# Three quarters of the first feed-forward product computed from seven block products instead of eight

## The chip, the cores and the metric

The kernel runs on one core of a Trainium2 chip. The metric is the device time of one execution in microseconds (us), so less is better. The engines of the core are named as in the profile: PE (matrix products; PEld is its weight load), DVE (VectorE, elementwise work), ACT (ScalarE, activations, copies and casts), POOL (GpSimd) and SP (which only issues DMAs here). Each has a queue of its own and works it off in order; semaphores tie the queues together.

## What is computed

One inference step of a two-layer network on 640 tokens (128 prompt tokens and 512 sample tokens), D = 1024 and a feed-forward width of 4096. A layer is a mixer (one wide projection, four branches, their gates, an output projection) and then a feed-forward block:

```python
h = _rmsnorm(x, g_pre_ffn) * (1 + sc2) + sh2
f = jnp.square(jax.nn.relu(h @ w_ff1)) @ w_ff2
x = x + gt2 * _rmsnorm(f, g_post_ffn)
```

The scale, shift and gate vectors (`sc1`, `sh2`, `gt2` and so on) come from `silu(cond) @ w_ada + b_ada`, for two conditioning vectors.

## The kernel before

**Precision.** Every fp32 operand x of a product is split: `hi` is x cast to fp32r, `lo` is x - hi. A product is three matmuls: hi by hi, hi by lo, lo by hi (`mm3`, L205).

**Weights.** All weights of the two layers are cut into 264 units of 128x1024, 132 for each layer. A unit is fetched by SP into one of three raw buffers (`wr`), ACT casts it to `wh` (L160), DVE subtracts to get `wl` (L170). Four pairs of `wh`/`wl` (`N_SETS`) exist, so the unit in use and the three that follow it can be ready at once (`w_pump`, `w_low`, `w_next`, `w_done`).

**Feed-forward.** `ffn` (L1106) goes over the 4096 columns in four quarters c = 0 to 3. In a quarter, the "ff stage" makes 8 blocks of 128 columns, each in two halves of 320 tokens: 24 matmuls of 128x320 (8 blocks of the contraction by 3), then ACT takes Relu out of PSUM (L1117) and Square into `ghi` (L1118), and DVE squares again and subtracts to get `glo` (L1119, L1120). The "nat stage" (`natural`, L565) then multiplies the 1024 columns by `w_ff2`: 8 units of 30 matmuls of 128x512, the results added into `f` by DVE (L578). In quarter 0 the norm of the last tokens is still being finished inside the ff stage.

**Side work.** The conditioning products are done on DVE, a chunk of 512 columns at a time: 16 accumulations of 128x512 per chunk (L413, L415), 20 chunks in all, then an all-reduce over the partitions on POOL. They are a generator (`ada`), and so is other side work (convolution, pooling, attention). `tick(pe, dve)` is called after each group of matmuls: it adds `pe - dve` to a credit, and generators run as long as the credit is above zero. It then makes one `wl` (`w_low(1)`). `need` runs `ada` to the point where a given vector is there.

**What sets the order.** The program is written in the order of emission; each engine takes its instructions in that order (manual schedule). PSUM has two groups of four buffers (`mm` and `sd`). Tiles of 128x640 come from a pool of 27 (`T`).

Of the kernel before, what the change touches and what calls it, by code (L numbers as in the profile page):

```python
# [27 lines left out]
TICKS = 5  # L28
NAT_TICK = ((1.2, 0), (0.9, 0), (0.1, 0), (0.6, 0.6))
FF_DVE = 0.8  # L30
KN = {'l_pl': 2, 'ws': 0.0, 'l_brow': 2, 'l_red': 2, 'l_red2': 2, 'l_q': 2, 'l_last': 3, 'l_mean': 3, 'l_var': 3, 'l_rb': 4, 'l_ub': 2, 'sec': 0.5, 'gp': 0.1, 'bp': 0.75, 'qs': 2.0, 'qkv': 0, 'j0': -2, 'pv': 0.5, 'sc': 0.5, 'cv': 1.5}
# [38 lines left out]
class Kernel:  # L70
# [35 lines left out]
    def add(self, name, gen, unit, steps):  # L106
        self.sides.append(Side(name, gen, self.l * N_UNITS + unit, steps))
# [31 lines left out]
    def w_init(self):  # L139
        self.w_dma = 0  # L140
        self.w_split = 0
        self.w_at = 0
        self.w_live = 0
        self.w_raw = {}
        self.w_raw_live = 0
        self.w_late = []
        self.w_set = {}

    def w_pump(self, upto):
        nc = self.nc  # L150
        total = L * N_UNITS
        while self.w_split <= min(upto, total - 1) and self.w_live < N_SETS:
            i = self.w_split
            if i not in self.w_raw:
                self.w_low()
            self.w_fetch(i)
            raw = self.w_raw.pop(i)
            hi = self.wp.tile([128, 1024], F32R, tag="wh", name=self.nm("wh"), bufs=N_SETS)
            lo = self.wp.tile([128, 1024], F32R, tag="wl", name=self.nm("wl"), bufs=N_SETS)
            nc.scalar.copy(hi, raw)  # L160
            self.w_set[i] = (hi, lo)
            self.w_late.append((i, raw, hi, lo))
            self.w_split += 1
            self.w_live += 1

    def w_low(self, n=None, upto=None):

        while self.w_late and (n is None or n > 0) and (upto is None or self.w_late[0][0] <= upto):
            i, raw, hi, lo = self.w_late.pop(0)
            self.nc.vector.tensor_tensor(lo, raw, r32(hi), ALU.subtract)  # L170
            self.credit -= W_DVE
            self.w_raw_live -= 1
            self.w_fetch(i + N_RAW)
            n = None if n is None else n - 1

# [11 lines left out]
    def w_next(self):  # L187
# [3 lines left out]
        self.w_low(upto=i)  # L191
# [367 lines left out]
    def x_load(self, t, src, bufs=3):  # L559
# [5 lines left out]
    def natural(self, hi, lo, f, mode, ch=None):  # L565
# [5 lines left out]
        for n in range(2):  # L571
# [37 lines left out]
            for j in range(4):  # L609
                u, st = self.w_next()  # L610
                for t in range(NT):
# [5 lines left out]
                    self.tick(*NAT_TICK[j])  # L617
# [487 lines left out]

    def ffn(self, hi, lo, f, ch):  # L1106
        nc = self.nc
        for c in range(4):
# [13 lines left out]
            order = [(i, h) for i in range(8) for h in range(2)]  # L1122
            if c == 0:
# [264 lines left out]
```

## Time and profile before

| | us |
|---|---|
| three runs, lowest / median / highest | 2076.58 / 2079.00 / 2079.83 |
| the profiled execution | 2085.78 |
| its span, first to last instruction | 2083.9 |
| PE busy in the span | 2031.3 (97%) |
| DVE busy | 1305.9 (63%) |
| ACT busy | 787.1 (38%) |
| POOL busy | 286.3 (14%) |

The profiled execution lies 6.8 us above the median of the runs. PE's matmuls overlap, so its busy share says that matmuls were in flight, not that the array was at its peak. In the span, layer 0's feed-forward lies at 603 to 1062 us and layer 1's at 1621 to 2084. The stages of a quarter alternate: ff, nat, ff, nat.

### The profile page before, as it was taken

The page shows a single profiled execution, that of the slowest core. Times are in us where ns is not written, and L with a number is a line of the kernel's source. Part 1 is how long each engine was busy: PE and PEld are TensorE (multiplying, and loading weights), DVE is VectorE, ACT ScalarE, POOL GpSimd, SP SyncE. Part 2 cuts the span into 40 slices and gives each one's busy share as a digit, 9 for nine tenths or more (in the row PEclk, how much of TensorE's full clock was granted, in tenths as well). Part 3 has the DMA queues.
Part 4 walks back from the last instruction along what each step waited for, and adds up shares of the span by engine and source line. Part 5 has one row for each costly group of instructions (what it writes and reads, how often), then busy time and mean ns, then how long its engine had stood idle before and what let it go on. Part 6 is the DMA issues. An engine that isn't in the chain of part 4 may idle for free.

```text
span 2083.9 us, 30694 instructions
## 1 busy us (share of the span) xinstructions
PE 2031.3 (97%) x12368; PEld 1884.0 (90%) x12368; DVE 1305.9 (63%) x2293; ACT 787.1 (38%) x1538; POOL 286.3 (14%) x213
## 2 busy tenths in 40 slices
PE   7999999899999999999989999999999999999998
PEld 4999999899889898989889999889998889989896
DVE  4678785578678385656776898666434863333344
ACT  4433445433263241313354344455324523223231
POOL 1203001013231123121241030100001211000000
PEclk9999999999999999999999999999999999999999
DMA  7332121233434243343534222112224442222222
GB/s 298 121 111 79 63 67 35 86 117 122 152 130 164 92 148 126 102 137 123 168 115 134 71 75 72 56 53 96 72 72 152 135 138 81 80 72 78 74 103 80
DMA packets 77935, 221.41 MB, mean 106 GB/s; under 512 B 11224, under 2 KB 12248, under 8 KB 77792
## 3 DMA queue, kind: packets, MB, share of 16 engines
q1 hardware_dynamic: 48160, 164.00, 23.2%
q10 hardware_dynamic: 28096, 55.34, 8.0%
q8 instruction: 97, 1.59, 0.3%
q0 software_dynamic: 1536, 0.10, 0.2%
q14 instruction: 46, 0.38, 0.1%
HBM read 208.61 MB, written 10.80 MB: 105 GB/s over the span
## 4 chain that ended last, share of the span: by engine, by line
PE 83%; DVE 7%; ACT 5%; issue 2%; DMA 1%; POOL 1%; ACTq 0%; SPq 0%; DVEq 0%; POOLq 0%
PE nat L208 8%; PE nat L210 8%; PE nat L209 8%; PE ff L213 7%; PE ff L214 7%; PE ff L212 7%; PE gp L212 6%; PE gp L213 6%; PE gp L214 6%; PE sec L212 3%; PE sec L214 3%; PE sec L213 3%; PE bp L212 2%; PE bp L214 2%; PE bp L213 2%; DVE wl L170 2%
## 5 line engine op out<-in xcount | busy, mean ns | idle before, releaser
L170 DVE TENSOR_TENSOR wl<-wr,wh 128x1024 fp32r<-128x1024 f32 x264 | 349.8, 1328 | 215.9 <-ACT wh L160 215.5
L160 ACT CAST wh<-wr 128x1024 fp32r<-128x1024 f32 x264 | 274.2, 1045 | 369.5 <-PE nat L210 305.3
L212 PE MATMUL gp<-hhi,wh 128*128 128x320 f32 x1024 | 321.6, 314 | 3.1 <-ACT sg L1076 2.2
L213 PE MATMUL ff<-hlo,wh 128*128 128x320 f32 x1024 | 317.4, 310 | 3.9 <-DVE hlo L540 2.7
L213 PE MATMUL gp<-hlo,wh 128*128 128x320 f32 x1024 | 319.1, 312 | 0.0
L214 PE MATMUL gp<-hhi,wl 128*128 128x320 f32 x1024 | 318.9, 311 | 0.0
L214 PE MATMUL ff<-hhi,wl 128*128 128x320 f32 x1024 | 317.2, 310 | 1.3 <-DVE wl L170 1.3
L212 PE MATMUL ff<-hhi,wh 128*128 128x320 f32 x1024 | 317.5, 310 | 0.0
L208 PE MATMUL nat<-wh,ghi 128*128 128x512 f32 x640 | 252.9, 395 | 0.0
L209 PE MATMUL nat<-wl,ghi 128*128 128x512 f32 x640 | 252.3, 394 | 0.0
L210 PE MATMUL nat<-wh,glo 128*128 128x512 f32 x640 | 252.3, 394 | 0.0
L427 POOL PARTITION_ALL_REDUCE red<-acc x40 | 147.0, 3719 | 741.5 <-DVE acc L415 390.0
L415 DVE SCALAR_TENSOR_TENSOR acc<-wa,silu_c,acc 128x512 f32<-128x512 f32 x280 | 196.8, 759 | 7.9 <-DMA wa<-in_wada_dram 7.8
L212 PEld LDWEIGHTS gp<-hhi,wh 128*128 128x128 f32 x1024 | 195.1, 191 | 4.9 <-ACT sg L1076 2.4
L213 PEld LDWEIGHTS ff<-hlo,wh 128*128 128x128 f32 x1024 | 192.9, 188 | 5.3 <-issue 3.4
L213 PEld LDWEIGHTS gp<-hlo,wh 128*128 128x128 f32 x1024 | 194.7, 190 | 1.3
L214 PEld LDWEIGHTS gp<-hhi,wl 128*128 128x128 f32 x1024 | 194.7, 190 | 0.0
L214 PEld LDWEIGHTS ff<-hhi,wl 128*128 128x128 f32 x1024 | 192.8, 188 | 1.8 <-DVE wl L170 1.8
L212 PEld LDWEIGHTS ff<-hhi,wh 128*128 128x128 f32 x1024 | 192.8, 188 | 0.3
L1076 ACT ACTIVATE sg<-gp 128x320 f32<-128x320 f32 x128 | 55.5, 434 | 294.7 <-PE gp L214 276.9
L1119 DVE TENSOR_TENSOR r<-r 128x320 f32<-128x320 f32 x128 | 62.6, 489 | 156.6 <-ACT ghi L1118 156.5
L1117 ACT ACTIVATE r<-ff 128x320 f32<-128x320 f32 x128 | 56.0, 438 | 248.1 <-PE ff L214 231.3
(204 smaller groups left out, 3782.8 us busy)
## 6 DMA issues: line engine op xcount, KB each, us to landing
wr<-in_wu_dram SPq DMA_DIRECT2D x264, 512.0 KB, 3.2
wa<-in_wada_dram ACTq DMA_DIRECT2D x160, 256.0 KB, 3.1
wa<-in_wada_dram SPq DMA_DIRECT2D x16, 512.0 KB, 8.6
x<-x ACTq DMA_DIRECT2D x15, 512.0 KB, 3.3
x<-x SPq DMA_DIRECT2D x15, 512.0 KB, 5.6
x<-in_x_sample_dram SPq DMA_DIRECT2D x8, 512.0 KB, 6.8
gp<-in_g_post_dram ACTq DMA_DIRECT2D x16, 256.0 KB, 3.2
out_dram<-x SPq DMA_DIRECT2D x10, 256.0 KB, 2.0
```

The costliest lines, as they stand in the source:

```text
L160: nc.scalar.copy(hi, raw)
L170: self.nc.vector.tensor_tensor(lo, raw, r32(hi), ALU.subtract)
L208: mm(out, lhsT=xhi, rhs=whi, start=start, stop=False)
L209: mm(out, lhsT=xhi, rhs=wlo, start=False, stop=False)
L210: mm(out, lhsT=xlo, rhs=whi, start=False, stop=stop)
L212: mm(out, lhsT=whi, rhs=xhi, start=start, stop=False)
L213: mm(out, lhsT=whi, rhs=xlo, start=False, stop=False)
L214: mm(out, lhsT=wlo, rhs=xhi, start=False, stop=stop)
L415: nc.vector.scalar_tensor_tensor(acc[c], w[k], s, acc[c], ALU.mult, ALU.add)
L427: nc.gpsimd.partition_all_reduce(red[c], acc[c], 128, bass_isa.ReduceOp.add)
L1117: nc.scalar.activation(r, ps[:, :HALF], AF.Relu)
L1119: nc.vector.tensor_tensor(r, r, r, ALU.mult)
```

## The change

Quarter 0 stays as it is. In quarters 1 to 3, units are taken in pairs (u, u+1), that is two blocks of 128 columns. The tokens are cut in two (p and q, 320 each), the contraction in two (4 blocks of 128 each), the columns in two (u and u+1): a 2x2 by 2x2 block product. It is made from seven block products (12 matmuls each, so 84 for 96), with sums of weight blocks, sums of token blocks, and sums of the results.

- **Weights.** A pair becomes four sets (`w_init`, `self.parts`): A = unit u; B = unit u+1 with its left half replaced by left plus right; C = two running sums over u's buffer; D = half a set, the last running sum. The sums are made in place in the raw buffers by DVE, four additions of 128x512 (`"sums"`, `"add22"`, `"add21"`). Casts and subtractions become two of 1024 and three of 512 columns for a pair, where there were two of 1024.
- **Tokens.** `ffn_acts` makes three sums and one replacement in place for each of four blocks, as side work in the nat stage of quarter 0: 14 DVE instructions of 128x320 and four casts on ACT a block. They lie in tiles of the `x` pool, which grows from three to four buffers, and of the `T` pool.
- **Results.** `ffn_pairs` is the new ff stage. Seven DVE instructions of 128x320 and one ACT copy gather the products out of PSUM; then Relu, Square and cast of 128x640 on ACT, and one subtraction of 128x640 on DVE, for each of the two blocks.
- **Side work.** While `ffn_pairs` runs, the credit is held at -1, so no generator runs. In the nat stages of the feed-forward the credit is 1.39 a tick (`FF_TICK`). `ab2` and `ab1` are needed later, in `late`, in the middle of the nat stage.

```diff
+FF_TICK = ((1.39, 0), (1.39, 0), (1.39, 0), (1.39, 0.7))
...
+                elif u % 2 == FF0 % 2:
+                    plan = [[(ALL, g, ALL, "sums")], [(ALL, g + 1, ALL, None)],
+                            [(LEFT, g, LEFT, "add22"), (RIGHT, g, LEFT, "add21")], [(LEFT, g, LEFT, "free")]]
...
+            v(lo, raw, r32(hi), ALU.subtract)
             self.credit -= W_DVE
-            self.w_raw_live -= 1
-            self.w_fetch(i + N_RAW)
+            if then == "sums":
+                self.w_fetch(u + 1)
+                x, y = self.w_raw[u], self.w_raw[u + 1]
+                v(x[:, LEFT], x[:, LEFT], y[:, LEFT], ALU.add)
+                v(y[:, LEFT], y[:, LEFT], y[:, RIGHT], ALU.add)
+            elif then == "add22":
+                v(raw, raw, self.w_raw[u + 1][:, RIGHT], ALU.add)
+                self.w_drop(u + 1)
+            elif then == "add21":
+                v(raw, raw, self.w_raw[u][:, RIGHT], ALU.add)
+            elif then == "free":
+                self.w_drop(u)
...
-    def x_load(self, t, src, bufs=3):
+    def x_load(self, t, src, bufs=4):
...
-                    self.tick(*NAT_TICK[j])
+                    self.tick(*(NAT_TICK if ch else FF_TICK)[j])
...
+        def square(j, x):
+            nc.scalar.activation(x, x, AF.Relu)
+            nc.scalar.activation(x, x, AF.Square)
+            nc.scalar.copy(ghi[j], x)
+            late.append((j, x))
+
+        def low():
+            j, x = late.pop(0)
+            v(glo[j], x, r32(ghi[j]), ALU.subtract)
+
+        for pr in range(4):
+            U, R = self.T("u"), self.T("r")
+            ps = {}
+            for ns in ((1, 2), (7, 3), (5, 6), (4,)):
+                u, st = self.w_next()
+                for i, n in enumerate(ns):
+                    w = ps[n] = (self.sdps if n in (7, 3, 5) else self.mmps)("ffp")[:, :HALF]
+                    for k in range(4):
+                        c = slice(i * 512 + k * 128, i * 512 + k * 128 + 128)
+                        self.mm3(w, st[0][:, c], st[1][:, c], *acts[n][k], k == 0, k == 3)
+                    if n == 1:
+                        nc.scalar.copy(U[:, p], w)
+                    elif n == 2:
+                        v(R[:, p], w, U[:, p], ALU.add)
+                    elif n == 6:
+                        v(U[:, p], w, U[:, p], ALU.add)
+                        v(R[:, q], ps[7], U[:, p], ALU.add)
+                        v(U[:, q], ps[5], R[:, q], ALU.subtract)
+                        v(U[:, p], ps[5], U[:, p], ALU.subtract)
+                        v(U[:, p], ps[3], U[:, p], ALU.add)
+                        square(2 * pr + 1, U)
+                    elif n == 4:
+                        v(R[:, q], w, R[:, q], ALU.add)
+                        square(2 * pr, R)
+                    if late and n in (2, 3):
+                        low()
+                    self.credit = -1.0
+                    self.tick(0, 0)
+                self.w_done(u)
...
+            if c:
+                self.drain("sums")
+                self.ffn_pairs(hi, lo, S, ghi, glo)
+                order = []
...
+            if c == 0:
+                self.add("sums", self.ffn_acts(hi, lo, S), FF0 + 14, 12)
...
     def late(self):
         if self.ab:
-            self.A, self.B = self.k.make_ab(*self.ab)
+            self.k.need(*self.ab)
+            self.A, self.B = self.k.make_ab(*self.k.res[self.ab])
```

How the order moves. DVE in the ff stage of layer 0, quarter 1, before (`r` and `glo` are the squared block and its low part, `acc` the conditioning sums, `wl` the low part of the next weights):

```order
L1119 TENSOR_TENSOR r_7644<-r_7644 128x320 [waits Activation_49]
L1120 TENSOR_TENSOR glo_7409<-r_7644,ghi_7401 128x320 [waits DVE_49]
L415 SCALAR_TENSOR_TENSOR acc_7488<-wa_7573,silu_c,acc_7488 128x512 [waits DMAHW4_49]
L415 SCALAR_TENSOR_TENSOR acc_7487<-wa_7573,silu_c,acc_7487 128x512
L415 SCALAR_TENSOR_TENSOR acc_7488<-wa_7593,silu_c,acc_7488 128x512 [waits DMAHW5_49,DVE_49]
L415 SCALAR_TENSOR_TENSOR acc_7487<-wa_7593,silu_c,acc_7487 128x512 [waits DVE_49]
L170 TENSOR_TENSOR wl_7652<-wr_7435,wh_7651 128x1024 [waits PE_49,Activation_49]
L1119 TENSOR_TENSOR r_7684<-r_7684 128x320 [waits Activation_49]
```

The same engine and place now, from the products of the second pair (`u_7632` and `r_7633` gather them; `wl_7741` is set C of the third pair, in two halves, `wl_7770` its set D):

```order
L1219 TENSOR_TENSOR u_7632<-ffp_7719,u_7632 128x320 [waits PE_49]
L1220 TENSOR_TENSOR r_7633<-ffp_7670,u_7632 128x320 [waits DVE_49]
L1221 TENSOR_TENSOR u_7632<-ffp_7705,r_7633 128x320 [waits DVE_49]
L1222 TENSOR_TENSOR u_7632<-ffp_7705,u_7632 128x320
L1223 TENSOR_TENSOR u_7632<-ffp_7688,u_7632 128x320 [waits DVE_49]
L197 TENSOR_TENSOR wl_7741<-wr_7552,wh_7740 128x512 [waits Activation_49]
L205 TENSOR_TENSOR wr_7552<-wr_7552,wr_7610 128x512 [waits DVE_49]
L1226 TENSOR_TENSOR r_7633<-ffp_7748,r_7633 128x320 [waits PE_49]
L197 TENSOR_TENSOR wl_7741<-wr_7552,wh_7740 128x512 [waits Activation_49]
L208 TENSOR_TENSOR wr_7552<-wr_7552 128x512 [waits DVE_49]
L197 TENSOR_TENSOR wl_7770<-wr_7552,wh_7769 128x512 [waits Activation_49]
```

The accumulations are gone from the stage, and the low parts of set C now stand between the gathering of the products and a sum that the next cast reads.

ACT in the same two places, before (a Relu out of PSUM, a Square, and now and then a whole cast of the next weights):

```order
L1117 ACTIVATE r_7684<-ff_1312_7654 128x320 [waits PE_49]
L1118 ACTIVATE ghi_7402<-r_7684 128x320 [waits Activation_49]
L1117 ACTIVATE r_7714<-ff_1315_7689 128x320 [waits PE_49]
L1118 ACTIVATE ghi_7402<-r_7714 128x320 [waits Activation_49]
L160 CAST wh_7719<-wr_7510 128x1024 [waits DMAHW7_49]
```

And now:

```order
L188 CAST wh_7702<-wr_7610 128x1024 [waits DMAHW1_49,DVE_49,PE_49]
L1195 ACTIVATE u_7632<-u_7632 128x640 [waits DVE_49]
L1196 ACTIVATE u_7632<-u_7632 128x640 [waits Activation_49]
L1197 CAST ghi_7486<-u_7632 128x640 [waits Activation_49]
L188 CAST wh_7740<-wr_7552 128x512 [waits PE_49]
L188 CAST wh_7740<-wr_7552 128x512 [waits DVE_49]
L1195 ACTIVATE r_7633<-r_7633 128x640 [waits DVE_49]
L1196 ACTIVATE r_7633<-r_7633 128x640 [waits Activation_49]
L1197 CAST ghi_7485<-r_7633 128x640 [waits Activation_49]
L188 CAST wh_7769<-wr_7552 128x512 [waits DVE_49,PE_49]
```

Casts of weights that waited for a DMA or for nothing now wait for DVE, and stand behind activations that wait for DVE too.

## Rows read from the trace of the kernel before

**Rows 1.** The page, part 1: busy time and share of the span.

```profile
PE 2031.3 (97%) x12368; PEld 1884.0 (90%) x12368; DVE 1305.9 (63%) x2293; ACT 787.1 (38%) x1538; POOL 286.3 (14%) x213
```

**Rows 2.** Stretches: start:end, length, each engine's busy us (instructions), PEclk, DMA share, GB/s.

```profile
665.90:721.80 55.90, 55.90 (x243) 45.18 (x242) 23.68 (x30) 14.38 (x19) 6.75 (x2) 1.00 0.35 119
721.80:778.20 56.40, 56.40 (x386) 56.40 (x385) 41.02 (x61) 22.07 (x39) 10.51 (x6) 1.00 0.43 137
...
1740.40:1796.70 56.30, 56.30 (x386) 56.30 (x385) 24.62 (x39) 21.76 (x39) 0.00 (x0) 1.00 0.24 80
1796.70:1852.60 55.90, 55.90 (x242) 45.03 (x241) 16.57 (x19) 9.21 (x10) 0.00 (x0) 1.00 0.22 76
```

**Rows 3.** Groups of DVE by form, 1740.4 to 2021.0 us: busy, mean ns | idle before.

```profile
L170 DVE TENSOR_TENSOR wl<-wr,wh 128x1024 fp32r<-128x1024 f32 x40 | 49.0, 1225 | 51.6 <-ACT wh L160 51.6
L1120 DVE TENSOR_TENSOR glo<-r,ghi 128x320 fp32r<-128x320 f32 x47 | 23.1, 492 | 1.6
```

**Rows 4.** The same view, all of the span: the nearest forms on DVE.

```profile
L1228 DVE TENSOR_TENSOR f<-f,G 128x512 f32<-128x512 f32 x20 | 13.3, 680 | 0.0
L234 DVE TENSOR_TENSOR zl<-ot,zh 128x640 fp32r<-128x640 f32 x8 | 6.1, 821 | 4.7 <-ACT zh L233 4.7
L1035 DVE TENSOR_TENSOR sc<-sec,sc 128x320 f32<-128x320 f32 x8 | 3.9, 483 | 1.6 <-PE sec L214 1.6
```

**Rows 5.** The same view, all of the span: the nearest forms on ACT.

```profile
L160 ACT CAST wh<-wr 128x1024 fp32r<-128x1024 f32 x264 | 274.2, 1045 | 369.5 <-PE nat L210 305.3 <-DVE acc L415 18.3 <-DVE acc L413 11.3
L739 ACT CAST pth<-PT 128x512 fp32r<-128x512 f32 x60 | 34.3, 585 | 28.4 <-PE PT L737 26.5 <-DVE cv L821 1.7
L1034 ACT COPY sc<-sec 128x320 f32<-128x320 f32 x8 | 3.4, 426 | 15.4 <-PE sec L214 15.4
L839 ACT ACTIVATE sq<-cv 128x640 f32<-128x640 f32 x4 | 2.7, 730 | 2.5 <-DVE cv L835 2.5
```

**Rows 6.** Instructions in order of time, in the ff stage of layer 0, quarter 2: start, us.

```profile
855.62 0.47 ACT L1118 ACTIVATE ghi<-r 128x320 fp32r<-128x320 f32 x1
856.00 1.04 ACT L160 CAST wh<-wr 128x1024 fp32r<-128x1024 f32 x1
856.13 0.49 DVE L1119 TENSOR_TENSOR r<-r 128x320 f32<-128x320 f32 x1 [2.50 <-ACT ghi L1118]
856.66 0.49 DVE L1120 TENSOR_TENSOR glo<-r,ghi 128x320 fp32r<-128x320 f32 x1
857.07 1.23 DVE L170 TENSOR_TENSOR wl<-wr,wh 128x1024 fp32r<-128x1024 f32 x1
```

**Rows 7.** Groups of DVE by form, 721.8 to 1002.2 us, where POOL works too.

```profile
L170 DVE TENSOR_TENSOR wl<-wr,wh 128x1024 fp32r<-128x1024 f32 x39 | 55.3, 1419 | 24.3 <-ACT wh L160 24.3
L1120 DVE TENSOR_TENSOR glo<-r,ghi 128x320 fp32r<-128x320 f32 x46 | 28.4, 617 | 1.6
```

**Rows 8.** The page, part 6: the weights' DMA, KB each, us to landing.

```profile
wr<-in_wu_dram SPq DMA_DIRECT2D x264, 512.0 KB, 3.2
```

**Rows 9.** Stretches: the mixers of layer 0 and layer 1, columns as in rows 2.

```profile
86.60:543.30 456.70, 443.57 (x2961) 433.82 (x2960) 336.28 (x647) 188.44 (x389) 55.31 (x43) 0.99 0.27 88
1113.70:1563.10 449.40, 442.54 (x2960) 433.19 (x2959) 306.24 (x609) 189.15 (x389) 34.78 (x27) 0.99 0.23 76
```

**Rows 10.** The same two stretches, the accumulations of L415 alone (DVE busy, count).

```profile
86.60:543.30 456.70, 44.58 (x65) 0.99 0.27 88
...
1113.70:1563.10 449.40, 19.35 (x28) 0.99 0.23 76
```

**Rows 11.** Stretches around PE's longest wait of the span, columns as in rows 2.

```profile
1062.00:1066.70 4.70, 1.49 (x12) 1.20 (x11) 4.56 (x9) 2.23 (x5) 0.60 (x1) 0.99 0.31 107
1066.70:1070.10 3.40, 3.40 (x19) 3.40 (x18) 2.65 (x8) 2.48 (x5) 0.55 (x1) 0.51 0.85 291
1070.10:1073.50 3.40, 3.40 (x31) 3.40 (x31) 2.30 (x5) 1.84 (x7) 1.46 (x1) 1.00 0.55 200
```

More of the change, by code (lines that the diff above doesn't have):

```diff
@@ L106, in add @@
     def add(self, name, gen, unit, steps):
-        self.sides.append(Side(name, gen, self.l * N_UNITS + unit, steps))
+        self.sides.append(Side(name, gen, self.set0[self.l] + unit, steps))
     def drain(self, *names):
@@ L139, in w_init @@
     def w_init(self):
+        self.parts, self.set_part, self.set0 = [], [], []
+        for l in range(L):
+            self.set0.append(len(self.set_part))
+            for u in range(N_UNITS):
+                g = l * N_UNITS + u
+                if u < FF0 + 16 or (u - FF0) % 16 >= 8:
+                    plan = [[(ALL, g, ALL, "free")]]
+                elif u % 2 == FF0 % 2:
+                    plan = [[(ALL, g, ALL, "sums")], [(ALL, g + 1, ALL, None)],
+                            [(LEFT, g, LEFT, "add22"), (RIGHT, g, LEFT, "add21")], [(LEFT, g, LEFT, "free")]]
+                else:
+                    plan = []
+                for p in plan:
+                    self.set_part.append(len(self.parts))
+                    self.parts += [(len(self.set_part) - 1, *x) for x in p]
+        self.set_part.append(len(self.parts))
         self.w_dma = 0
@@ L150, in w_pump @@
         nc = self.nc
[L151 to L154, printed above, removed]
-                self.w_low()
[L156 to L159, printed above, removed]
+        while self.w_split < len(self.parts) and self.parts[self.w_split][0] <= upto:
+            i, c, u, rc, then = self.parts[self.w_split]
+            if i not in self.w_set:
+                if self.w_live >= N_SETS:
+                    break
+                self.w_set[i] = [self.wp.tile([128, 1024], F32R, tag=n, name=self.nm(n), bufs=N_SETS) for n in ("wh", "wl")]
+                self.w_live += 1
+            if u not in self.w_raw:
+                self.w_low()
+            while any(x[1] in (u, u - 1) for x in self.w_late):
+                self.w_low(1)
+            self.w_fetch(u)
+            raw = self.w_raw[u][:, rc]
+            hi, lo = [w[:, c] for w in self.w_set[i]]
@@ L174, in w_low, with w_drop @@
+            self.w_fetch(u + N_RAW)
             n = None if n is None else n - 1
+    def w_drop(self, u):
+        del self.w_raw[u]
+        self.w_raw_live -= 1
     def w_fetch(self, upto):
@@ L1106, in ffn @@
     def ffn(self, hi, lo, f, ch):
         nc = self.nc
+        S = {n: [] for n in range(1, 5)}
         for c in range(4):
```

65 lines of the change are left out of this document (52 added, 13 removed).

## The prediction

> **What bounds it now.** I read the page first: PE has matmuls in flight for 97% of the span, DVE works 63%, ACT 38% [rows 1]. Then the stretches, cut at the stages: in an ff stage of quarters 1 to 3 PE is busy for all of its 56.3 to 56.4 us (six stages; the first and the fourth stand there), in the nat stages for all of 55.6 to 55.9 us [rows 2]. So PE sets these stages alone. An ff stage is 384 matmuls of 128x320, so one is issued every 56.35 / 384 = 0.1467 us. DVE has slack there: 24.6 us of work in a stage of layer 1, 41.0 in one of layer 0, where the conditioning sums and POOL run too [rows 2]. Last I looked at what follows what on DVE and ACT, since the change makes long chains there: a step that waits for the other engine starts 0.03 to 0.04 us after it (0.47 us from 855.62, next engine at 856.13); one that needs the step before it on its own engine starts 0.04 after its end (856.13 + 0.49, then 856.66); one that doesn't starts about 0.08 before its end (856.66 + 0.49, then 857.07) [rows 6].
>
> **What is removed.** 4 pairs by 3 quarters by 2 layers is 24 pairs, each with 12 matmuls fewer: 288 by 0.1467 = 42.3 us, 7.05 a stage. A stage has 28 products of 12 matmuls, 1.76 us each: 49.3 us if PE never waits.
>
> **What is added, as busy time.** Prices: DVE 1.23 us for 1024 columns [rows 3], 0.68 for 512, 0.82 for 640 and 0.48 for 320 out of PSUM [rows 4]; ACT 1.05 for 1024, 0.59 for 512, 0.73 for 640, 0.43 for 320 out of PSUM [rows 5]. A pair on DVE: 2 by 1.23, 3 by 0.68, 4 sums by 0.68, 7 gatherings by 0.48, 2 low parts by 0.82: 12.2 us, against 12.3 us of matmuls. On ACT: 2 by 1.05, 3 by 0.59, 0.43, 6 by 0.73: 8.7 us. By busy time alone it just fits.
>
> **What is added, as a chain.** It doesn't fit, because the two engines wait for each other in turn. The order shows the lap, from the gathering after product 6 of one pair to that of the next:
> - five gatherings on DVE, four of them in a chain: 2.45;
> - Relu, Square and cast of the block on ACT: 2.3;
> - the cast of C's left half, which stands behind these on ACT (0.5), its subtraction on DVE (0.7) and the sum into the raw buffer (0.7): 1.95 with the handoffs;
> - the cast of C's right half, which reads that sum: 0.6;
> - Relu, Square and cast of the other block: 2.2;
> - the cast of D behind them: 0.5;
> - on DVE D's low part, the gathering of product 2, the first block's low part: 1.8;
> - A's low part and two sums: 2.45;
> - the cast of B, which reads the second sum, and its low part: 2.3.
>
> Together 16.55 us, for 12.3 us of matmuls. PE enters a stage with four sets ready, so it isn't stopped at once. The first gathering starts when six products are out: 6 by 1.76 + 0.2 = 10.8 us into the stage. The second starts at 27.3, the third at 43.9. C of the third pair is ready 6 us after the second (2.45 + 2.3 + the cast and subtraction), at 33.4, where PE wants it at 2 by 12.3 + 4 by 1.76 = 31.7: the first wait. From there PE follows the lap. The last pair prepares the first unit of the nat stage in place of A, ready after all but the last two terms and the sums, 10.0 + 1.8 + 1.2 = 13.0 us into the third lap: 56.9. So the ff stage ends at about 57.0 and not at 49.3: 7.7 us are lost where 7.05 were won. The fourth token tile of the nat stage then takes the PSUM buffer of product 4, which DVE reads some 17.6 us after the third lap's start (the last lap is 1.9 shorter, without sums): about 61.5 to 62, where PE comes at 57.0 + 3 by 1.4 = 61.2. I take 0.4. Sum of a stage: -7.05 + 7.7 + 0.4 = +1.05; six stages +6.3 us. The weights' DMA lands in 3.2 us [rows 8], and a raw buffer is free about 6 us before the sum that reads its next unit, so I cost the DMA at nothing; a landing twice as slow would begin to lengthen the lap.
>
> **The clock.** After PE's longest wait the granted clock fell to 0.51 (1.2 GHz) for 3.4 us, with 19 matmuls where the next 3.4 us had 31 [rows 11]. The waits of a stage, 1 to 2 us at product 5 and shorter ones behind it, are in that class. A half-clock stretch costs at most 1.7 us, and nothing where PE then waits anyway. Bounds 0 and 1.7 a stage; I take 0.5, since most of it should lie in later waits: +3 us, at most +10.
>
> **What moves.** No conditioning sum runs in the six ff stages now. By the order, 96 of the 320 accumulation steps stand between the conditioning columns of layer 1's two norms, that is mostly in layer 1's mixer, where 42 stood. The nearest rows are layer 0's mixer, 65 accumulations (of L415 alone) in 456.7 us, and layer 1's, 28 in 449.4 [rows 9, 10]. So the 54 steps cost between 0 and 7.3 us; I take 3.5, since the two mixers also differ in how they begin. The nat stage of quarter 0 gets the token sums, 56 by 0.48 = 27 us on DVE; 23.7 of 55.9 us are taken now [rows 2], part of it sums that leave: covered, at nothing. If ACT's turns in it used up the cover, the first lap would start late, by no more than a few us twice.
>
> **Sum.** 2085.8 (profiled execution) - 42.3 + 6 by 8.1 + 3 + 3.5 = 2098.6, 12.8 more than before. The profiled execution was 6.8 above the median, so on the runs 2079.0 + 12.8 = about 2092.
>
> **Rivals.**
> 1. PE stays the bound and the lap is hidden. For it: DVE at 63% and ACT at 38% [rows 1]. Against it: the lap has only one instruction in flight most of the time, so shares say little. Price: 2079.0 - 42.3 + 3.5 = 2040. With the mixer's and the clock's terms it decides on the length of the lap: a stage ends at 10.8 + 2.79 laps, so it breaks even at a lap of about 15.8 us, and the whole gain needs about 13.8.
> The Trainium skill, "Perfetto Trace Analysis", section "Identifying the Most-Contended Engine", has the engine with the highest occupancy optimized first; taken as the forecast, that gives this rival's 2040. The trace of before agrees that TensorE is that engine (97% against 63%), but no row of before has DVE and ACT in such a chain.
> 2. The lap is some 5 to 10% shorter than I added up, because starts overlap more. A lap of 15.2 ends the stage at 53.2: -2.8 a stage, 2079.0 - 6 by 2.8 + 6.5 = 2069; a lap of 16.0 gives about 2083. Every term is from a measured form, so 5% is what I grant.
> 3. It is longer. Beside POOL the same subtraction took 1419 ns for 1225 and 617 for 492 [rows 3, 7]; POOL's reductions now fall into the nat stages, but may run over. A lap 5% longer adds 2.3 a stage, the clock's upper end 7 and the mixer's 4 more: up to 2117.
>
> **How the numbers follow.** A measurement can tell about 0.2%, 4 us. Chances: the lap as added up, 2083 to 2104, 0.58; rival 1, 0.10; rival 2, 0.20, of which half is faster by over 0.2% and half within; rival 3, 0.12. Some 0.01 more for faster and 0.04 for the same come from the forecast's lower edge: faster 0.21, same 0.14, slower 0.65. The range must leave out at most 0.2: rival 1 and the top of rival 3 are left out, so 2066 to 2112.
>
> **What would show it.** In the changed profile the first two pairs of an ff stage run without a wait of PE; product 5 of the third pair waits for DVE's `wl` or ACT's `wh`, and so does product 5 of the fourth; two gatherings after product 6 stand about 16.5 us apart; the stage lasts 57 us, not 49. PE's waits in the six stages add up to some 45 us. If a stage lasts 49 to 51 us, the lap is wrong and rival 1 holds. If the stages last 57 and the total is still lower, the gain lies elsewhere, in the mixers or at the changes of stage, and the terms for what moves are wrong.

## Result and profile after

The changed kernel takes 2097.52 us (median of 4 runs, 2094.31 to 2099.6), the kernel before beside it 2079.41 (4 runs, 2076.58 to 2082.56). The ratio is 1.0085, 95% interval 1.0066 to 1.0105: the change makes the kernel slower, by 18 us where 13 were forecast. The profiled execution of the changed kernel took 2097.92 us with a span of 2096.2.

The first part of the page of the changed kernel answers to [rows 1]: busy time and share of the span.

```profile
PE 2013.9 (96%) x12080; PEld 1848.1 (88%) x12080; DVE 1487.6 (71%) x2597; ACT 867.7 (41%) x1618; POOL 293.9 (14%) x213
```

288 matmuls are gone and PE is busy 17 us less, yet the span grew. The shares hardly show why; the stretches do. Columns as in [rows 2]; the stages of the changed kernel: a new feed-forward stage of layer 0, the last natural stage of layer 0, and a pair of stages of layer 1 (feed-forward, natural).

```profile
716.40:773.40 57.00, 53.09 (x337) 50.73 (x336) 36.52 (x56) 28.46 (x41) 0.00 (x0) 0.97 0.19 59
1004.20:1071.90 67.70, 61.59 (x266) 49.49 (x265) 46.89 (x87) 30.07 (x65) 20.48 (x17) 0.95 0.40 141
1747.30:1804.20 56.90, 52.42 (x338) 49.26 (x336) 36.40 (x56) 28.48 (x41) 0.00 (x0) 1.00 0.18 58
1804.20:1861.20 57.00, 56.26 (x242) 44.92 (x242) 30.71 (x38) 13.69 (x16) 9.02 (x2) 1.00 0.31 100
```

In a new stage of layer 1 PE is busy 52.4 us of 56.9, where it was busy for all of 56.3 [rows 2]. What it waits for in that stage (engine and line, what ended the wait: us in total, times, longest), 1747.3 to 1804.2:

```profile
PE ffp L254 <- ACT wh L188: 3.3, 4, 1.7
PE ffp L256 <- DVE wl L197: 0.9, 5, 0.2
```

And what VectorE waits for there:

```profile
DVE wl L197 <- ACT wh L188: 19.4, 14, 3.6
```

And the lap itself, as ScalarE's instructions in order of time in that stage (start, us; in brackets the idle time before and what ended it):

```profile
1760.55 0.74 ACT L1195 ACTIVATE u<-u 128x640 f32<-128x640 f32 x1 [4.65 <-DVE u L1223]
1761.32 0.74 ACT L1196 ACTIVATE u<-u 128x640 f32<-128x640 f32 x1
1762.09 0.73 ACT L1197 CAST ghi<-u 128x640 fp32r<-128x640 f32 x1
1762.73 0.62 ACT L188 CAST wh<-wr 128x512 fp32r<-128x512 f32 x1
1764.83 0.62 ACT L188 CAST wh<-wr 128x512 fp32r<-128x512 f32 x1 [1.49 <-DVE wr L205]
...
1777.40 0.74 ACT L1195 ACTIVATE u<-u 128x640 f32<-128x640 f32 x1 [3.67 <-DVE u L1223]
...
1794.24 0.74 ACT L1195 ACTIVATE u<-u 128x640 f32<-128x640 f32 x1 [3.67 <-DVE u L1223]
```

VectorE's instruction that needs the cast of 1762.73:

```profile
1763.38 0.69 DVE L197 TENSOR_TENSOR wl<-wr,wh 128x512 fp32r<-128x512 f32 x1 [2.86 <-ACT wh L188]
```

The Relu of one pair and that of the next stand 16.85 and 16.84 us apart, for 12.3 us of matmuls. Behind each Relu come Square and cast, and only then, at 1762.73, the cast of the next weight block that DVE's chain needs. ACT then idles for DVE (1.49, 3.67) and DVE for ACT (2.86 here, 19.4 us in the stage).

Where the time went, stage by stage, from the start of one stage's first matmul to that of the next. There are two profiles of each kernel (`before2` and `after2` below are the second ones, with spans of 2076.8 and 2093.4). All four stand in the table, since one profile of a kernel differs from another by more than some terms are worth.

| stretch, us | before | before2 | changed | after2 | predicted difference |
|---|---|---|---|---|---|
| start to the end of layer 0's mixer | 543.3 | 540.4 | 538.0 | 535.1 | 0 |
| natural, ff and natural of quarter 0, layer 0 | 178.4 | 178.5 | 178.3 | 178.3 | 0 |
| three new ff stages, layer 0 | 169.0 | 169.0 | 174.2 | 174.1 | +2.0, clock +1.5 |
| two natural stages behind them | 111.4 | 111.4 | 113.6 | 113.5 | +0.8 |
| last natural stage of layer 0 | 59.9 | 59.9 | 67.7 | 68.0 | +0.4 |
| q, k, v and mixer, layer 1 | 501.1 | 496.9 | 499.0 | 499.3 | +3.5 |
| natural, ff, natural of quarter 0, layer 1 | 177.2 | 177.1 | 176.4 | 176.4 | 0 |
| three new ff stages, layer 1 | 168.9 | 168.9 | 170.9 | 170.7 | +2.0, clock +1.5 |
| natural stages behind them, to the end | 174.6 | 174.6 | 178.0 | 178.0 | +1.2 |

From `before2` to `after2` the rows add up to 16.6 us: the six new stages 6.9, the five natural stages behind them (all but the last of layer 0) 5.4, the last natural stage of layer 0 8.1, and -3.8 elsewhere: -5.3 up to the end of layer 0's mixer, +2.4 in layer 1's q, k, v and mixer, -0.9 in the two stretches of quarter 0. Two of these, the 8.1 and the -5.3, no step of the prediction had.

In the last natural stage of layer 0, which took 59.9 before, PE waits 5.6 us at one place, for the transposes of a norm (`xn`):

```profile
PE hT L553 <- ACT xn L537: 5.6, 1, 5.6
```

VectorE there, in order of time, in the changed kernel:

```profile
1017.52 4.06 DVE L457 SCALAR_TENSOR_TENSOR acc<-wa,silu_c,acc 128x512 f32<-128x512 f32 x6
...
1041.37 0.18 DVE L425 TENSOR_TENSOR A<-mc,cols 128x16 f32<-128x16 f32 x1 [5.77 <-DMA mc<-mrow]
```

and POOL's queue beside it:

```profile
1021.67 8.49 POOL L469 PARTITION_ALL_REDUCE red<-acc  x2 [80.27 <-DVE acc L457]
1030.04 1.04 POOL L479 DMA_DIRECT2D mrow<-red  x2
1032.84 0.81 POOL L482 DMA_DIRECT2D mc<-mrow  x1 [1.77 <-DMA mrow<-red]
1036.63 0.77 POOL L482 DMA_DIRECT2D mc<-mrow  x1 [2.98 <-issue]
```

The last conditioning sums of layer 1's first columns end at 1021.6, 17 us into the stage. All-reduce, the trip to memory and the trip back then follow one after the other, and the columns are there 19.8 us later, at 1041.4. VectorE, which has come to the instruction that needs them, waits 5.77 us with the sums and norms of all token tiles queued behind it. The transposes of those norms are what PE waits for. Behind its wait the granted clock falls, which adds to the loss:

```profile
1050.00:1056.90 6.90, 5.51 (x17) 4.74 (x18) 5.21 (x13) 4.83 (x12) 1.51 (x3) 0.51 0.55 210
1056.90:1063.70 6.80, 6.80 (x35) 5.62 (x35) 5.16 (x9) 4.06 (x12) 3.50 (x4) 1.00 0.02 8
```

At a granted clock of 0.51 there are 17 matmuls, in the next stretch of that length 35.

### The profile page after: what moved, and what is told of

It is laid out like the page before. It is cut to its first block, busy times and chain, and to the rows that moved or that the text cites. A ratio compares the mean times of both kernels' runs of the same rounds, so it can differ in the third digit from the quotient of the medians.

```text
span 2096.2 us, 30622 instructions
## 1 busy us (share of the span) xinstructions
PE 2013.9 (96%) x12080; PEld 1848.1 (88%) x12080; DVE 1487.6 (71%) x2597; ACT 867.7 (41%) x1618; POOL 293.9 (14%) x213
## 4 chain that ended last, share of the span: by engine, by line
PE 65%; DVE 17%; ACT 9%; issue 4%; DMA 3%; POOL 2%; ACTq 0%; DVEq 0%; SPq 0%; POOLq 0%
PE nat L250 7%; PE nat L252 7%; PE nat L251 7%; PE gp L254 6%; PE gp L255 6%; PE gp L256 6%; DVE wl L197 5%; ACT wh L188 3%; PE sec L254 2%; PE sec L256 2%; PE sec L255 2%; PE bp L254 2%; PE bp L256 2%; PE bp L255 2%; DMA wa<-in_wada_dram 2%
## 5 line engine op out<-in xcount | busy, mean ns | idle before, releaser
L197 DVE TENSOR_TENSOR wl<-wr,wh 128x1024 fp32r<-128x1024 f32 (+1 forms) x336 | 392.0, 1172 | 251.6 <-ACT wh L188 249.7
L188 ACT CAST wh<-wr 128x1024 fp32r<-128x1024 f32 (+1 forms) x336 | 318.9, 958 | 371.9 <-PE nat L252 168.7
L250 PEld LDWEIGHTS nat<-wh,ghi 128*128 128x128 f32 x640 | 120.7, 189 | 32.9 <-DVE r L1226 5.2
L251 PEld LDWEIGHTS nat<-wl,ghi 128*128 128x128 f32 x640 | 120.6, 188 | 30.7 <-DVE wl L197 2.9
L252 PEld LDWEIGHTS nat<-wh,glo 128*128 128x128 f32 x640 | 120.6, 188 | 28.6
L863 DVE SCALAR_TENSOR_TENSOR cv<-val,wch,cv 128x113 f32<-128x113 f32 (+14 forms) x240 | 125.1, 588 | 0.1
L256 PE MATMUL ffp<-hhi,wl 128*128 128x320 f32 x384 | 120.2, 313 | 2.4 <-DVE wl L197 2.4
L254 PE MATMUL ffp<-hhi,wh 128*128 128x320 f32 x384 | 119.2, 311 | 1.4 <-ACT wh L188 1.4
L254 PE MATMUL sec<-hhi,wh 128*128 128x320 f32 x384 | 119.8, 312 | 0.0
L256 PE MATMUL sec<-hhi,wl 128*128 128x320 f32 x384 | 118.6, 309 | 0.0
```

The lines of the kernel that those rows point to most:

```text
L197: v(lo, raw, r32(hi), ALU.subtract)
L250: mm(out, lhsT=xhi, rhs=whi, start=start, stop=False)
L251: mm(out, lhsT=xhi, rhs=wlo, start=False, stop=False)
L252: mm(out, lhsT=xlo, rhs=whi, start=False, stop=stop)
L254: mm(out, lhsT=whi, rhs=xhi, start=start, stop=False)
L256: mm(out, lhsT=wlo, rhs=xhi, start=False, stop=stop)
```

## Experiments

### The order alone (`order`)

The same instructions; only their order on ScalarE and the place of the blocks' low parts are other. The three activations of a block are put aside and issued behind the casts of the next weights.

```diff
+        held = []
+
         def square(j, x):
-            nc.scalar.activation(x, x, AF.Relu)
-            nc.scalar.activation(x, x, AF.Square)
-            nc.scalar.copy(ghi[j], x)
-            late.append((j, x))
+            held.append(lambda: nc.scalar.activation(x, x, AF.Relu))
+            held.append(lambda: nc.scalar.activation(x, x, AF.Square))
+            held.append(lambda: (nc.scalar.copy(ghi[j], x), late.append((j, x))))
+
+        def go(n):
+            for _ in range(min(n, len(held))):
+                held.pop(0)()
...
                 u, st = self.w_next()
+                go({4: 1, 1: 2, 7: 3}.get(ns[0], 0))
...
-                    if late and n in (2, 3):
-                        low()
                     self.credit = -1.0
                     self.tick(0, 0)
+                    if late and n in (7, 3):
+                        low()
                 self.w_done(u)
+        go(6)
```

> The same instructions as the changed kernel, in another order: in the new ff stages ACT's casts of the next weights (C, then D, then A) go ahead of the activations of the block just gathered, and DVE makes the low parts of both blocks after the sums of the next pair. Theory L (the stages are set by the lap in which DVE and ACT wait for each other, 16.85 us in the changed kernel): the lap loses the three activations twice and comes to 13 to 13.5 us by the same durations; PE then hardly waits, the six stages take 49.5 to 51 us each, the whole 2050 to 2062. Theory D (DVE is simply full, some 12.2 us of work for 12.3 us of matmuls, plus what it loses between instructions): the work is the same, the stages stay at 56 to 59 us and the whole at 2094 to 2100.

Measured: 2056.59 us (4 runs, 2051.41 to 2061.94), ratio 0.9865 (0.984 to 0.989), as theory L had it. The new stages of layer 1 last 49.3 us from the start of one stage to the next, those of layer 0 up to 50.7. The stretch of one of them, columns as above, in `order`:

```profile
1729.60:1778.90 49.30, 49.30 (x338) 49.26 (x336) 35.31 (x55) 25.39 (x38) 0.00 (x0) 1.00 0.22 71
```

PE is busy for all of it: 28 products of 1.76 us, as the prediction had it for a stage without waits. ScalarE now, in order of time:

```profile
1744.21 0.62 ACT L188 CAST wh<-wr 128x512 fp32r<-128x512 f32 x1 [3.29 <-DVE wr L205]
1744.73 0.73 ACT L1197 ACTIVATE u<-u 128x640 f32<-128x640 f32 x1
1746.39 0.62 ACT L188 CAST wh<-wr 128x512 fp32r<-128x512 f32 x1 [0.92 <-DVE wr L208]
1746.91 0.73 ACT L1198 ACTIVATE u<-u 128x640 f32<-128x640 f32 x1
...
1759.25 0.73 ACT L1197 ACTIVATE u<-u 128x640 f32<-128x640 f32 x1
```

Cast and activation alternate, and the lap is 14.52 us (1744.73 to 1759.25) for 16.85; the 13 to 13.5 that theory L added up for it were too few. So it was the order on the queues that cost, not the amount of work (the new place of the low parts on VectorE was not tried without ScalarE's new order): with not one instruction less, 41 us went by the medians, 46 by the ratios to before's runs. The Trainium skill, "Perfetto Trace Analysis", section "Tensor Engine Instruction (MATMUL, LD_WEIGHTS)", states that ScalarE, VectorE and GpSimd take their instructions strictly in the order of their queues; the two orders of ScalarE shown here agree with it: in the changed kernel a cast stands behind activations that nothing on PE is waiting for (1760.55 to 1762.73), and in `order` the Relu of 1744.73, whose input VectorE had finished at 1742.85, stands behind a cast that waits 3.29 us.

What comes next is seen in the natural stage behind it, 58.5 us long; its waits in `order` from 1778.8 to 1838:

```profile
PE nat L250 <- DVE r L1232: 0.7, 1, 0.7
PE nat L251 <- DVE wl L197: 0.7, 1, 0.7
PE nat L250 <- DVE u L1225: 0.7, 1, 0.7
```

### One activation more, or two sums more (`act_pad`, `dve_pad`)

To see which of the two engines carries the lap, each got work of its own: ScalarE a second Relu on both blocks of a pair, VectorE two maxima of 640 columns behind the five gatherings.

```diff
             nc.scalar.activation(x, x, AF.Relu)
+            nc.scalar.activation(x, x, AF.Relu)
             nc.scalar.activation(x, x, AF.Square)
```

> Each Relu of a 128x640 block is done twice (the second changes nothing): 2 x 0.74 us of ACT more per pair, ACT at some 10.3 of 12.3 us. Theory L: both stand in the lap, which grows from 16.85 to about 18.3 us; a stage ends some 2.8 laps after its first gathering, so it grows by 4 us to 61 to 62, the whole by 25 us to about 2122. Theory D: ACT has room, nothing changes beyond 3 us.

```diff
                         v(U[:, p], ps[3], U[:, p], ALU.add)
+                        for _ in range(2):
+                            v(R, R, R, ALU.max)
                         square(2 * pr + 1, U)
```

> Two DVE instructions of 128x640 that change nothing (a block's maximum with itself) are put behind each set of five gatherings, where DVE waits for ACT's cast by the profile: 1.6 us of DVE more per pair. Theory L: they lie in a wait of 2.9 us, the lap stays at 16.9, the stages within 0.5 us of 57 to 59, the whole within 4 us. Theory D: DVE has 13.8 us of work for 12.3, a stage grows by 4 to 6 us, the whole by 25 to 36.

Measured: `act_pad` 2121.67 us in one run; each of its new stages of layer 1 lasts 61.4 us for 56.9 to 57.1 in the changed kernel. Two pads of 0.77 us lengthen the lap by 1.5 us, three laps by 4.5, and the stage by 4.3 to 4.6: all of ScalarE's added time comes through. ScalarE in `act_pad`, in order of time:

```profile
1788.94 0.74 ACT L1195 ACTIVATE u<-u 128x640 f32<-128x640 f32 x1 [3.67 <-DVE u L1224]
...
1807.30 0.74 ACT L1195 ACTIVATE u<-u 128x640 f32<-128x640 f32 x1 [3.67 <-DVE u L1224]
```

A lap of 18.36, with ScalarE's wait for DVE the same 3.67. `dve_pad`: 2107.97 us in one run; its new stages last 57.0, 56.8 and 56.8 in layer 1, unchanged, though VectorE has as much more to do. At that place it waits for ScalarE anyway. That the whole would stay within 4 us, as theory L added, missed: the span grew by 10.0. The five natural stages behind new ones (all but the last of layer 0) are 1.8 to 3.3 us longer each, 13.7 in all, and their first token tiles wait for the last pair's gatherings; the last natural stage of layer 0 is 3.6 shorter.

### More conditioning sums in the natural stages (`tick`)

```diff
-FF_TICK = ((1.39, 0), (1.39, 0), (1.39, 0), (1.39, 0.7))
+FF_TICK = ((1.5, 0), (1.5, 0), (1.5, 0), (1.5, 0.7))
```

> One number changed: the credit of a tick in the feed-forward's nat stages is 1.5 instead of 1.39, so the conditioning sums for layer 1 run earlier. Theory (the nat stage of layer 0, quarter 3, is 7.8 us longer because the last conditioning columns land after the middle of the stage, where they are needed now): DVE's wait for that DMA shrinks by the time that the last sums move up; if they move up by 5 us or more the stage falls from 67.8 to 61 to 62 us and the whole by 6 us, to about 2091. Rival (the wait comes from the x loads, which now wait for buffers that hold the token sums): the stage stays at 67 to 68. The six ff stages stay as they are by both, 57 to 59.

Measured: 2100.22 us, ratio 1.0092 (1.0063 to 1.0121), so no gain; the expectation failed. The last natural stage of layer 0 fell only from 67.7 to 64.4, and the one behind quarter 1 rose from 56.7 to 64.5. The latter's waits, 790 to 830, in `tick`:

```profile
PE nat L250 <- DVE f L620: 4.6, 2, 3.0
```

L620 empties PSUM into `f`; the added sums stand ahead of it on VectorE. What the columns gained by coming earlier, PE paid for its PSUM buffers. That the late columns are the cause of the 8 us was therefore still open.

### Fewer sums in the last chunk (`few_sums`)

Ten of the sixteen accumulations of the last chunk of these columns are left out, so its output is not the reference's; all else is the changed kernel.

```diff
+        K = 3 if (l, ch) == (1, 3) else 8
-        for k in range(-3, 8):
+        for k in range(-3, K):
             n = k + 3
-            if n not in w and n < 8:
+            if n not in w and n < K:
```

> The changed kernel with ten of the sixteen accumulations left out of the last chunk of the conditioning columns for layer 1 (its sums are therefore wrong by five eighths of the terms); all else as it is. Theory M (late columns): the last natural stage of layer 0 is 67.8 us long in the changed kernel because the last of these accumulations end at 1021.5, and all-reduce, two trips to memory and the columns' use follow one after the other; with ten fewer the chunk ends before that stage begins, the wait of 5.6 us on TensorE goes, the stage falls to 60 or 61 and the kernel from 2097.5 to 2089-2091 (7 to 8 less). Rival V (volume): the stage is long since VectorE has more to do in it; ten accumulations of 0.6 us are 6 us of work of which few lie on the path: stage 65 to 67, kernel 2095-2097.

Measured: 2086.62 us (10 runs), ratio 1.0013 (0.9999 to 1.0026). The stage, columns as above:

```profile
1005.70:1066.80 61.10, 59.53 (x266) 47.29 (x265) 44.32 (x84) 29.67 (x64) 9.47 (x11) 1.00 0.48 172
```

61.1 us for 67.7. PE's wait for the norm is 0.6 for 5.6, and the granted clock stays at 1.00, where it was 0.95. VectorE's work in the stage fell only by 2.6 us (44.3 for 46.9), less than the stage did: it is the time at which the columns come, not the volume, as theory M has it. By ratios the kernel gained 15 us beside before's runs, by the two medians 11; the stage has 6.6 of it, where theory M had put 7 to 8 on the whole. Another 5.3 lie in layer 1's q, k, v stage and mixer (493.7 us from the start of the one to the end of the other, 499.0 in the changed kernel), with 90 accumulations there for 96. Why six fewer are worth that much was not looked into.

### PSUM buffers of the natural stages (`psum`)

`order`, with the buffers of the first token tiles taken so that none is one that the last pair's gatherings still read.

```diff
-                        ps[t] = self.mmps("nat") if t < 4 else self.sdps("nat")
+                        ps[t] = self.mmps("nat") if t < 4 - 2 * (mode == "add") or t == 4 and mode == "add" else self.sdps("nat")
```

> The version with the new order of ScalarE (order, 2056.6) and one change more: in the natural stages after pairs the first two PSUM buffers come from the one group, the third and fourth from the other, so that the first four token tiles don't ask for a buffer that the last pair's gatherings still read. Theory P: the three waits of 0.7 us at the head of each of these stages are waits for PSUM buffers, two go, and the stages fall from 58.7 to 57.0-57.3; six stages, so 2047-2050. Rival W: the waits are for the weights' low parts and the queue behind them on VectorE, which this doesn't touch: stages stay at 58.4-58.8, kernel 2055-2058.

Measured: 2048.12 us (2045.61 to 2050.04), ratio 0.984 (0.9818 to 0.9861). The natural stages behind new stages are 56.7 to 56.8 us long (apart from the last of each layer, which has other work), and of the three waits only the one for `wl` is left, 0.7 us. Theory P holds. The last natural stage of layer 0 is still 67.8.

### Sums inside the new stages (`fill`, `fill2`)

`psum`, with one conditioning step (two accumulations) in each of the first three pairs of a stage; in `fill2` only in the first two pairs, and in layer 0 alone.

```diff
-                    self.credit = -1.0
+                    self.credit = 0.1 if n == 5 and pr < 3 else -1.0
```

> psum with one change more: one conditioning step (two accumulations, some 1.2 us of VectorE) in each of the first three pairs of a feed-forward stage, where the changed kernel has none. Theory L (the pair is bound by TensorE once ScalarE's order is mended, and VectorE has 1.6 us to spare in each, as dve_pad showed): the feed-forward stages stay at 49.5-50.5, the columns of layer 1 come in time and the last natural stage of layer 0 falls from 67.9 to 60-61: 7 less than psum, some 2041-2044. Rival F (VectorE's room is used up by the shorter pair of 12.4 us): the stages of layer 0 grow by 1.2 us a pair, 3.6 each, which gives back more than the columns bring: 2046-2050.

```diff
-                    self.credit = -1.0
+                    self.credit = 0.1 if n == 5 and pr < 2 and self.l == 0 else -1.0
```

> fill with its conditioning steps only in the first two pairs and only in layer 0 (fill: 2042.6 beside before's 2085.0, ratio 0.9815). Theory F2: the wait of 1.6 us for a weight's low part in the fourth pair of fill's second and third new quarter of layer 0 is VectorE's room used up, and goes with the third step: those stages fall from 51.6 and 52.1 to 50.0-50.5, the columns are still in time (last natural stage 61): ratio 0.979-0.980. Rival C: twelve accumulations for eighteen are too few, the columns come late again, the stage is 63-66 and the ratio 0.982-0.984.

Measured: `fill` 2042.62 us (2040.42 to 2043.26), ratio 0.9815 (0.9792 to 0.9838); `fill2` 2042.7, ratio 0.9822 (0.9793 to 0.9851). They can't be told apart; `fill` is 5.5 us below `psum`, which ran beside it. Two stretches of `fill`, the last natural stage of layer 0 and the new stage of quarter 2, and below them the first of these in `fill2`, from two answers:

```profile
981.10:1042.20 61.10, 59.49 (x265) 47.42 (x265) 49.50 (x85) 32.75 (x68) 19.31 (x17) 1.00 0.49 167
820.20:872.00 51.80, 49.99 (x338) 49.24 (x336) 43.41 (x69) 24.69 (x37) 0.00 (x0) 1.00 0.27 86
```

```profile
981.20:1047.00 65.80, 60.72 (x265) 48.71 (x265) 46.81 (x87) 32.85 (x69) 20.50 (x17) 0.97 0.46 155
```

In `fill` the columns come in time (61.1 us), and VectorE's room is used up in two stages of layer 0, where PE waits 1.6 us for a weight's low part. In `fill2` that wait is gone, but the stages only fall to 50.9 and 51.6 from start to start, not to the 50.0 to 50.5 of F2, and the columns are late again, 65.8. So `fill` has L's gain in the natural stage and part of F's loss, and `fill2` came out as rival C had it. `fill` also shows that volume is not the cause of the long natural stage: VectorE has more to do there (49.5 us for 46.9 in the changed kernel), and the stage is 6.6 us shorter. `fill` is faster than the kernel before by 1.9%; with `fill2` it is the best version here.

### The changed kernel again, and without its new rule elsewhere (`before2`, `after2`, `rule`)

The changed planner has a rule that the low parts of a raw block and of the one before it go ahead of its next cast. It holds everywhere, not only in the new pairs. `rule` holds it to those.

```diff
-            while any(x[1] in (u, u - 1) for x in self.w_late):
+            while u % N_UNITS >= FF0 + 16 and any(x[1] in (u, u - 1) for x in self.w_late):
```

> The kernel before once more, unchanged, for a second profile. Theory N (noise): the end of layer 0's first mixer, 543.3 in the first profile and 538.0 in the changed kernel's, differs from profile to profile by some us without any edit: it falls at 535-541 here, and the span is 2077 rather than 2083.9. Rival E (edit): it stays at 543 within 0.7, and the 5 us are brought by the changed order of the weights' low parts in the mixer.

> The changed kernel once more, beside the two below on one chip: 2095-2100, ratio 1.007-1.010; its last natural stage of layer 0 is 66-68 again and the pairs are 16.8 long. If that stage differs by over 2 us, the late columns are no fixed cost.

> The changed kernel with its new rule on the order of the weights' low parts (those of the same raw block or the one before go before its next cast) held to the blocks of the new pairs; elsewhere the order is that of the kernel before. Theory M (the rule helps the mixers): TensorE's idle 3.1 us between 200 and 300 of the kernel before, which the changed kernel hasn't, comes back, and the first mixer ends at 540-543 for 538: 2 to 5 more than after2, 2099-2103. Rival N (noise): the mixers differ from profile to profile by as much, mostly with stretches at half clock, and the time is that of after2 within 2.

Measured: `before2` one run of 2078.68 us, with the natural stage behind the first mixer at 540.4; `after2` 2095.57 us, ratio 1.0072 (1.0047 to 1.0096), at 535.1; `rule` 2106.46 us, ratio 1.0129 (1.01 to 1.0157), at 540.7. The first two came out as expected, with 68.0 us again for the last natural stage of layer 0 in `after2`. On one chip the rule is worth 10.9 us, more than the 2 to 5 that theory M expected. Of the spans' 8.5 us between the two, 5.6 lie ahead of the first natural stage and 3.9 in layer 1's q, k, v stage and mixer (503.2 for 499.3); all else is 1.0 less. PE's waits in the first mixer, 85 to 545 us, first in `after2`, then in `rule`:

```profile
PE PT L779 <- ACT S L768: 3.7, 9, 1.3
PE O L791 <- DVE ptl L782: 2.7, 3, 1.6
PE bp L254 <- DVE macc L1138: 2.2, 1, 2.2
PE nat L250 <- DVE mt L1138: 1.7, 1, 1.7
PE S L743 <- DVE cv L903: 0.9, 1, 0.9
```

```profile
PE PT L779 <- ACT S L768: 4.6, 11, 1.3
PE O L791 <- DVE ptl L782: 4.0, 2, 2.3
PE gp L254 <- ACT sg L1118: 2.2, 1, 2.2
PE gp L254 <- DVE macc L1138: 1.0, 1, 1.0
PE S L743 <- DVE cv L903: 0.9, 1, 0.9
```

The wait for `sg` is gone with the rule and others are shorter; one of `bp` for `macc` is new. The line for `mt` belongs to the natural stage behind the mixer, where `rule` has such a wait, of 0.9 us, just past this window. Without it the waits sum to 9.5 and 12.7 us, so they explain 3.2 of the 5.6. `rule` also has two half-clock stretches of 3.4 us in the mixer, `after2` one. Theory M holds by the times, and by its sign in the trace: between 200 and 300 us PE is idle for 3.1 us in `rule`, as before, and not at all in `after2`. That each wait moved by the rule's doing is not shown one by one. The first mixer alone doesn't settle it, since it varies without an edit: `order` and `act_pad` have the same instructions up to there, and enter the natural stage at 540.8 and 534.6. Their stretches, `order` first:

```profile
85.00:530.00 445.00, 435.51 (x2902) 426.05 (x2901) 327.12 (x634) 186.21 (x384) 55.93 (x43) 0.98 0.27 88
```

```profile
85.00:530.00 445.00, 435.65 (x2934) 426.32 (x2933) 333.00 (x643) 186.22 (x384) 56.13 (x43) 1.00 0.29 90
```

The granted clock was 0.98 in the one and 1.00 in the other, and 32 more matmul records stand in the same stretch: `order` has four half-clock stretches of 3.4 us there, `act_pad` one. `before2` and `after2` both have 1.00 there, `rule` 0.99; their 540.4, 535.1 and 540.7 compare better than any two with 0.98.

## Why the prediction came out right, and where its steps didn't

The forecast of 2092 us lay 5.5 below the measured 2097.5, inside its range, and its main mechanism is the one that the runs show. Part of the nearness is luck: two terms of 8 to 11 us that it didn't have cancel each other, and 3 us put down for the clock came from elsewhere.

- **The lap.** Predicted 16.55 us from single forms, measured 16.85. The sums in place took 0.69 us, the gatherings 0.48 to 0.49, the casts 0.62 and 1.05; only the cast of 512 columns was clearly off its nearest row, 0.62 for 0.59. Step by step, A's low part and the two sums behind it took 2.75 us for 2.45 (the steps wait for each other, where the prediction let them overlap) and each cast of 512 columns with its handoff 0.65 for 0.5; small differences the other way give 0.3 of this back. That the lap is on ScalarE's path, `act_pad` and `dve_pad` show from two sides, and `order` by taking it away.
- **Where PE waits.** Predicted at product 5 of the third and of the fourth pair, from 31.7 to 33.4 and then with the lap; measured 1.1 and 1.7 us at these two places (1779.1 and 1795.4, 31.8 and 48.1 us into the stage), none over 0.1 us in the first two pairs of layer 1's stages. Predicted end of the stage 57.0, measured 56.9 to 57.1 in layer 1. PE's waits and slack were put at 45 us for six stages; six stages of 56.9 to 58.7 us less 49.3 each give 49.3. The waits that the profile lists are only 24.8 of these: it counts PE as busy while a matmul is in flight, 0.31 us for one that is issued every 0.147.
- **The clock.** +3 predicted, 0 to 10 allowed; it cost some 1 us, and that the three stages of layer 0 fit the term is luck. Quarters 2 and 3 of layer 0 last 58.5 and 58.7, 1.4 to 1.8 more than the other four, and have half-clock stretches behind their waits. Three stretches of the changed kernel, around the first wait of such a stage:

```profile
861.00:865.70 4.70, 2.83 (x17) 2.31 (x17) 1.78 (x4) 2.73 (x4) 0.00 (x0) 1.00 0.00 0
865.70:869.10 3.40, 3.40 (x15) 3.40 (x14) 1.93 (x4) 3.15 (x6) 0.00 (x0) 0.50 0.47 153
869.10:872.50 3.40, 3.40 (x24) 3.16 (x23) 3.24 (x5) 1.37 (x3) 0.00 (x0) 0.99 0.44 141
```

  After a wait the granted clock is 0.50 (1.2 GHz) for 3.4 us, with 15 matmuls where the next 3.4 have 24. But the lap is 16.8 us in every stage, with a half clock or without, and what sets these two stages apart is there before the clock falls: the first Relu comes 14.6 and 14.8 us into the stage, in the other four 13.2 to 13.3. In `tick` the stage of quarter 2 is 58.0 us long at a granted clock of 1.00. VectorE at the head of quarter 2 of layer 0 (the stage starts at 830.1), and below it at the head of layer 1's first new stage (1747.3), from two answers:

```profile
834.88 1.41 DVE L457 SCALAR_TENSOR_TENSOR acc<-wa,silu_c,acc 128x512 f32<-128x512 f32 x2
836.20 0.69 DVE L197 TENSOR_TENSOR wl<-wr,wh 128x512 fp32r<-128x512 f32 x1
```

```profile
1748.65 0.69 DVE L197 TENSOR_TENSOR wl<-wr,wh 128x512 fp32r<-128x512 f32 x1 [3.59 <-ACT wh L188]
```

  Conditioning sums that the natural stage put into VectorE's queue, six in quarter 2 and eight in quarter 3, run on to 6 us into the new stage, and its first low part starts 6.1 us in, for 0.9 to 1.3 in the other four. So "no conditioning sum runs in the six ff stages now" is wrong for two of them. The prediction had a late first lap, for another reason, and at nothing. The 2.9 us of it in the two stages are a reading of the trace; no run moves these sums alone. What is left to the clock is some 0.2 us in each of the four stages that have a half-clock stretch behind the last long wait.
- **The natural stages behind the new ones.** Predicted +0.4 each, for the PSUM buffer of product 4; measured +0.9 to +1.4. That wait is there, 0.4, and in two of the five 0.3 for the first `wl`. The term was mis-sized, and the rest was not traced to single waits. It looked at one of the stage's first buffers; `order` shows, with the lap gone, three waits of 0.7, and `psum` removes two of them.
- **The conditioning sums.** The step that failed is "what moves". It counted where the accumulations go and priced those that fall into layer 1's mixer (96 by the order, 96 in the trace), at 0 to 7.3 us. That stretch came out between 2 below and 2 above before in the profiles at hand; `rule`, whose low parts there stand in before's order, is 2 to 6 above, so 3.5 was fair. But it didn't ask when the first layer-1 columns are needed. Before, their sums ran beside the ff stages, and the last natural stage of layer 0 took 59.9; in the changed kernel only what is left over from a natural stage runs in the next ff stage, the last chunk ends in the very stage that needs it, and 8 us are lost, to PE's wait and to the half clock behind it. `few_sums` shows this from one side and `fill` from the other.
- **The rule on the low parts.** The prediction gave it no term. It acts in the mixers too and won some 10 us there. Without it the change would have cost 27 us (2106.46 against 2079.85) and the forecast would have been 14 short.
- **The rivals.** Rival 1, PE the bound at 2040, fell for this kernel, with its condition: it asked for a lap under 13.8. It is where the mended versions come out (2042.6), though with a lap of 14.5: by the prediction's formula, 10.8 + 2.79 laps, such a stage would end at 51.3, and in `order` it ends at 49.3. In the other order the casts that PE needs come earlier in the lap, so the formula, made for the old order, doesn't hold there. The Trainium skill's "Identifying the Most-Contended Engine" ("Perfetto Trace Analysis") would have had PE's work as what to cut. PE had 97%, and 90% by its weight loads, which that section prefers for it [rows 1]. The change took 288 matmuls from it, 42 us at their pace, and the kernel got slower by 18: here the measurement goes against taking the rule as a forecast.

## What to carry to other kernels

When work is taken off the bounding engine and put as short steps on two others, add up the lap between those two from single instructions and the order of each queue; their busy shares (71% and 41% here) say nothing about it. Then look at what each in-order queue holds back: casts that the next matmuls need belong ahead of activations that nobody awaits yet, which here turned 0.9% slower into 1.4% faster without an instruction less. And for every piece of side work that loses its place, ask for its deadline, not only for its cost, and whether what is left of it stands ahead of the first instructions of the next stage.

## What was not expected of the hardware

The way of a conditioning chunk from its last sum to its use is 19.8 us, and of the computing engines only POOL works on it: two all-reduces 8.5, the way out to memory and back the rest, with 3 us between the issues of the two loads. The half clock behind a wait cost the lap nothing: in `act_pad` the three new stages of layer 1 are all 61.4 us long, with half-clock stretches of 6.8, 3.4 and 10.2 us in them. And the same instructions in the first mixer took 6 us more in one profile than in another, with a mean granted clock of 0.98 against 1.00: a single profile can't settle a term of that size in this kernel.
